# A two-layer flow-matching step: the correcting half of each weight is added from SBUF in convolutions and attention, from DRAM from the LayerNorm to the output projection

## The chip, the cores and the metric

The kernel runs on one core of a Trainium2 chip. The metric is the device time of one execution in microseconds (us), lower is better. The kernel before took 2286.52 us (median of 3 runs, 2286.14 to 2286.73).

## What is computed

Two layers of a backbone with four parallel branches (a Conformer convolution, a Hyena long convolution by FFT, a pooling mixer and grouped-query attention), on 128 context tokens and 512 latent tokens, all in float32. Cut to what matters here: nearly all the time goes into products of the 640 tokens with weight matrices.

```python
def parallel_mixer(h, p, latent, k_ctx, v_ctx):       # h: (1, L, 1024), L = 128 or 512
    u = h @ p['w_in']                                 # 1024 x 11264
    (a_glu, a_gate, b_proj, b_gate, c_in, c_gate,
     q, k, v, d_gate, g_merge) = jnp.split(u, points, axis=-1)
    ya = conformer_conv(a_glu, p['conv_dw_w'], p['conv_dw_b'], p['conv_ln_g'],
                        p['conv_ln_b'], p['conv_pw'])
    ya = (ya * jax.nn.silu(a_gate)) @ p['wo_conv']
    ...
    yb = hyena(b_proj, p['hy_short_w'], p['hy_short_b'], filt, p['hy_skip'])
    yb = (yb * jax.nn.silu(b_gate)) @ p['wo_hyena']
    yc = multiscale_pool(c_in, p['pool_w'], p['pool_scale'])
    yc = (yc * jax.nn.silu(c_gate)) @ p['wo_pool']
    ...
    yd = (att * jax.nn.silu(d_gate)) @ p['wo_attn']
    gm = jax.nn.sigmoid(g_merge).reshape(B, L, N_BRANCH, D_MODEL)
    merged = gm[:, :, 0] * ya + gm[:, :, 1] * yb + gm[:, :, 2] * yc + gm[:, :, 3] * yd
    return merged @ p['w_out'], k, v

def trunk_layer(x, cond, p, latent, k_ctx, v_ctx):
    mod = jax.nn.silu(cond) @ p['w_ada'] + p['b_ada']
    shift, scale, gate = jnp.split(mod, 3, axis=-1)
    h = rms_norm(x, p['norm_g']) * (1.0 + scale) + shift
    y, k, v = parallel_mixer(h, p, latent, k_ctx, v_ctx)
    return x + gate * y, k, v
```

## The kernel before

**Products in three parts.** A float32 number is split into a rounded high part and a remainder, each in the format that TensorE takes at its faster rate, and a product is the sum of three: weight high by activation high, weight high by activation remainder, weight remainder by activation high. Weights come in blocks of at most 128 x 1024 (512 KB). The generator `weights` (L333) makes the two halves of one block: SP loads the block from DRAM into the tile `raw` (L342), ACT casts it into `whi` (L343, in the trace a CAST), and then the remainder `wlo` is made in one of two ways. Where the flag `pooled[0]` is set, ACT writes minus `whi` into `wlo` (L346, an ACTIVATE), and a DMA that POOL issues adds the block to it once more (L347, an *add* below); its source is the weight in DRAM, so that it reads the block a second time, in runs of 512 bytes. Where the flag is not set, VectorE subtracts; that is so for the first three blocks alone, and 269 blocks have an add. `raw` has two buffers, `whi` and `wlo` three each.

**How a block is used.** `proj` (L386) runs, for each half of 320 tokens, 16 matmuls with `whi` and then 8 with `wlo` for a block of 1024 input channels (half as many for 512 channels, 2 and 1 for a block of `pool_w`). The result lies in one of three PSUM banks (`mm`), which ACT or VectorE empties.

**Stages of a layer.** Adaptive modulation; the Hyena branch with its filters, where TensorE runs input projections between the FFT products; values, keys, queries and attention; the merge of the Hyena branch during attention; the convolution's and the pooling branch's inputs; the merge of the attention branch (eight pairs of a `w_in` block and a `wo_attn` block); then `Pooling.gated` (L1737): four pairs of a `w_in` block of 512 KB and a `pool_w` block of 64 KB; the merge of the pooling branch; `Conv.gated` (L1651); the merge of the convolution; the output projection. `Conv.norm` (L1591), the LayerNorm of the convolution, runs on VectorE and ACT beside the attention merge and `Pooling.gated`, and ends inside the latter.

**What sets the order.** The program is written as generators (`lm.spawn`), and a small planner, `Loom`, picks the next one by estimated times; that fixes TensorE's order for good. On the other engines and on the DMA queues of SP and POOL, the tile framework orders the instructions by priority and by its own estimate of when they are ready; each engine then runs its list strictly in order, and waits on semaphores.

Of the kernel before, what the change touches and what calls it, by code (L numbers as in the profile page):

```python
# [10 lines left out]
F32R = mybir.dt.float32r  # L11
I32 = mybir.dt.int32
AF = mybir.ActivationFunctionType
ALU = mybir.AluOpType
# [51 lines left out]
def r32(ap):  # L66
    return ap.bitcast(F32)
# [165 lines left out]
def hybrid_flow_backbone(ctx: ExitStack, tc: tile.TileContext, i, o):  # L233
    nc = tc.nc
# [24 lines left out]
    def nm(p):  # L259
        count[0] += 1  # L260
        return f"{p}{count[0]}"
# [52 lines left out]
    def split(hi, lo, src, scale=None):  # L314
        if scale is None:
            act.copy(hi, src)
            dve.tensor_tensor(out=lo, in0=src, in1=r32(hi), op=ALU.subtract)
        else:
            act.activation(out=hi, in_=src, func=AF.Copy, scale=scale)
            dve.scalar_tensor_tensor(out=lo, in0=src, scalar=scale, in1=r32(hi),  # L320
                                     op0=ALU.mult, op1=ALU.subtract)
# [11 lines left out]
    def weights(src, kk, n):  # L333
        yield from wr.get()
        lm.bg = True
        with tc.high_priority(offset=WAHEAD):
            raw = wp.tile([P, 1024], F32, tag="raw", name=nm("raw"), bufs=NRAW)
            hi = wp.tile([P, 1024], F32R, tag="whi", name=nm("whi"), bufs=NHI)
            lo = wp.tile([P, 1024], F32R, tag="wlo", name=nm("wlo"), bufs=NHI)
            w = kk * n  # L340
            rv = raw[:, 0:w]
            sp.dma_start(out=rv.rearrange("p (k c) -> p k c", k=kk), in_=src)  # L342
            act.copy(hi[:, 0:w], rv)  # L343
            if pooled[0]:

                act.activation(out=lo[:, 0:w], in_=r32(hi[:, 0:w]), func=AF.Copy, scale=-1.0)  # L346
                nc.gpsimd.dma_start(out=lo[:, 0:w].rearrange("p (k c) -> p k c", k=kk), in_=src.bitcast(F32R),  # L347
                                    accum_op=ALU.add)
            else:
                dve.tensor_tensor(out=lo[:, 0:w], in0=rv, in1=r32(hi[:, 0:w]), op=ALU.subtract)  # L350
        lm.bg = False
        return (hi[:, 0:w].rearrange("p (k c) -> p k c", k=kk),
                lo[:, 0:w].rearrange("p (k c) -> p k c", k=kk))

    def w_cols(l, c0):
        return weights(i["w_in"][l][:, c0:c0 + 128].rearrange("(k p) c -> p k c", p=P), 8, 128)
# [18 lines left out]
    def slots(n, dt=F32):  # L375
        r = []
        for _ in range(n):
            r.append((yield from slot(dt)))
        return r

    def new_act(n):
        hi = yield from slots(n, F32R)
        lo = yield from slots(n, F32R)
        return Act(hi, lo)
# [69 lines left out]
    def rsqrt(out, v, n):  # L454

        t = sm.tile([P, 40], F32, tag="rsq_t", name=nm("rt"))[:, 0:n]
        dve.tensor_scalar(out=out.bitcast(I32), in0=v.bitcast(I32), scalar1=1, scalar2=None,
                          op0=ALU.logical_shift_right)
        dve.tensor_scalar(out=out.bitcast(I32), in0=out.bitcast(I32), scalar1=-1.0,
                          scalar2=1597463007.0, op0=ALU.mult, op1=ALU.add)  # L460
        for _ in range(3):
            dve.tensor_tensor(out=t, in0=out, in1=out, op=ALU.mult)
            dve.scalar_tensor_tensor(out=t, in0=t, scalar=-0.5, in1=v, op0=ALU.mult, op1=ALU.mult)
            dve.scalar_tensor_tensor(out=out, in0=t, scalar=1.5, in1=out, op0=ALU.add, op1=ALU.mult)
# [37 lines left out]
    def par(l, ct, row):  # L502
        return prm[:, ct, pcol(l, row):pcol(l, row) + 1]
# [150 lines left out]
    def ada_finish(l, p):  # L654

        ng = prm[:, 2 * (p % 2):2 * (p % 2) + 2, pcol(l, R_NG) + p // 2]
        for cnd in range(2):
            v = mods[l][:, 1, 2 * p:2 * p + 2, cnd]
            dve.scalar_tensor_tensor(out=v, in0=v, scalar=1.0, in1=ng, op0=ALU.add, op1=ALU.mult)
        ev_mod[l][p].set()  # L660
# [10 lines left out]
    def ada_later(jobs, step, start):  # L671
        yield lm.pe + start
        for l, j in jobs:
            yield from ada_chunk(l, j)
            if 4 <= j < 8:
                ada_finish(l, j - 4)
            yield lm.pe + step
# [158 lines left out]
    pooled = [False]  # L836
# [695 lines left out]
    class Conv:  # L1532
# [58 lines left out]
        def norm(self):  # L1591

            l = self.l
            yield self.ev_tap
            co = self.co
            pm = yield from sc.get()
            for j in range(2):
                pe.matmul(pm[:, j, 0:328], lnw.to_broadcast([P, P]), self.pad.v(328 * j, 328), start=True, stop=True)
            self.pad.free()
            for c in range(4):  # L1600
                x = co.v(656 * c, 656)
                xh = x.rearrange("p (a b) -> p a b", a=2)
                yield turn
                dve.tensor_tensor(out=xh, in0=xh, in1=pm[:, :, 0:328], op=ALU.subtract)
            sc.put()
            for c in range(4):
                sq = yield from ur.get(656)
                act.activation(out=sq, in_=co.v(656 * c, 656), func=AF.Square)
                if c == 0:
                    total = sq  # L1610
                else:
                    dve.tensor_tensor(out=total, in0=total, in1=sq, op=ALU.add)
                    ur.put()
            yield lm.sync()
            pvv = yield from ax.get()
            for t in range(5):
                t0 = 0 if t == 0 else 143 + 128 * (t - 1)
                pe.matmul(pvv[:, t:t + 1], total[:, t0:t0 + 128], lnw, start=True, stop=True)
            ur.put(0.0)
            v = sm.tile([P, 5], F32, tag="lnv", name=nm("lnv"))  # L1620
            rs = sm.tile([P, 5], F32, tag="lnr", name=nm("lnr"))
            dve.tensor_scalar(out=v, in0=pvv[:, 0:5], scalar1=EPS, scalar2=None, op0=ALU.add)
            ax.put()
            rsqrt(rs, v, 5)
            yield lm.sync()
            pr = yield from sc.get()
            for t in range(5):
                dst = pr[:, 1, 0:128] if t == 0 else pr[:, 0, 128 * (t - 1):128 * t]
                pe.transpose(dst, rs[:, t:t + 1].to_broadcast([P, P]), ident)
            self.sa = sa = yield from new_act(1)  # L1630
            for c in range(4):
                x = co.v(656 * c, 656)
                xn = yield from ur.get(T)
                dve.tensor_tensor(out=xn[:, 0:128], in0=x[:, 0:128], in1=pr[:, 1, 0:128], op=ALU.mult)
                yield turn
                dve.tensor_tensor(out=xn[:, 128:640], in0=x[:, 143:655], in1=pr[:, 0, :], op=ALU.mult)
                yield turn
                dve.tensor_scalar(out=xn, in0=xn, scalar1=par(l, c, R_LNG), scalar2=par(l, c, R_LNB),
                                  op0=ALU.mult, op1=ALU.add)
                th = yield from ur.get(T)  # L1640
                act.activation(out=th, in_=xn, func=AF.Tanh, scale=0.5)
                yield turn
                dve.scalar_tensor_tensor(out=xn, in0=th, scalar=1.0, in1=xn, op0=ALU.add, op1=ALU.mult)
                ur.put()
                split(sa.h(c), sa.l(c), xn, 0.5)
                ur.put()
            sc.put()
            co.free()
            self.ev_norm.set()

        def gated(self):  # L1651
            l = self.l
# [149 lines left out]
    def layers():  # L1802
# [4 lines left out]
        for l in range(DEPTH):  # L1807
# [74 lines left out]
            if l + 1 < DEPTH:  # L1882
                lm.spawn(late_filters(l + 1, ev_late[l]), 7)
                lm.spawn(ada_later([(1, j) for j in range(8, 12)], 0.0, GS), 50, LATA)
            if l + 1 < DEPTH:
                xT = yield from slots(2)
                evs = [Event(lm) for _ in range(4)]
            yield from out_proj(l, ma, xs, ssq, rows, xT, evs)
            for _ in range(2):
                ur.put()  # L1890
            ma.free()
            if l + 1 < DEPTH:
                yield evs[3]
# [11 lines left out]
    def late_filters(l, ev):  # L1905
        yield ev
        for q in range(2):
            hys[l].threads.append(lm.spawn(hys[l].filters(q), PF0))
# [41 lines left out]
    for x in DORD:  # L1950
# [3 lines left out]
        elif x in "fghi":  # L1954
            c, q = divmod("fghi".index(x), 2)
# [13 lines left out]
    lm.spawn(ada_first(chunks), 3)  # L1969
    lm.spawn(first_sums(*x_first), 4)  # L1970
    lm.spawn(layers(), 6)
    with tc.manual_schedule(engines={mybir.EngineType.PE}):
        lm.run()
# [94 lines left out]
```

## Time and profile before

| what | value |
|---|---|
| runs | 2286.14, 2286.52, 2286.73 us |
| the profiled execution's own time | 2285.64 us |
| its span (first to last instruction) | 2283.8 us, mean granted TensorE clock 0.984 |
| TensorE busy | 2192.5 us (96%) |
| VectorE, ScalarE, GpSimd busy | 58%, 52%, 26% |
| adds (queue q0) | 122.96 MB, 42.4% of the 16 DMA engines' time |
| loads and stores of SP (queue q1) | 186.19 MB, 27.3% |

The profiled execution is 0.9 us under the median. The names in a row of the trace are the kernel's tiles without their numbers: `wlo<-in_w_in_dram` on POOL is an add, `whi<-raw` on ACT a cast, `wlo<-whi` the negated copy, `mm<-sl,wlo` a run of matmuls with a remainder. In a row of a timeline the first number is the start in us from the span's start, the second the duration, and the bracket at the end tells how long the engine was idle before it and what ended that.

### The profile page before, as it was taken

To read this page: it belongs to the slowest core of one execution; us is meant where nothing else is said; L and a number is where in the kernel's file an instruction comes from. 1 tells how busy PE (TensorE), PEld (TensorE's weight loads), DVE (VectorE), ACT (ScalarE), POOL (GpSimd) and SP (SyncE) were. 2 spreads that over 40 slices of the span, in tenths; PEclk is the share of its full clock that TensorE was granted. 3 is DMA by queue.
4 is the path that set the end of the run, shared out by engine and by line. 5 is a ranking of instruction groups with operands and counts; after the bars stand their busy time and mean duration, and the time that the engine had idled before them with its cause. 6 is when DMAs were issued, how large, how long until landed. Compare 5 with 4: busy or idle time off the path is not lost.

```text
span 2283.8 us, 39935 instructions
## 1 busy us (share of the span) xinstructions
PE 2192.5 (96%) x15951; PEld 2145.5 (94%) x15951; DVE 1333.8 (58%) x2762; ACT 1190.4 (52%) x2169; POOL 590.2 (26%) x451
## 2 busy tenths in 40 slices
PE   5999999999999999999997999999999999999999
PEld 3899999999999999999987999999999999999999
DVE  5676786656679944122265777845766897522222
ACT  5544457667654335344564454656776543544442
POOL 2644321101112222222144353111111122222221
PEclk7899999999999999999998999999999999999999
DMA  9376766545568878899973656555455888698986
GB/s 280 104 159 143 163 141 122 101 79 104 109 126 146 151 123 151 150 168 167 226 185 73 109 106 123 105 101 98 82 109 102 150 150 150 113 164 148 173 169 137
DMA packets 508230, 311.83 MB, mean 137 GB/s; under 512 B 12760, under 2 KB 499352, under 8 KB 507789
## 3 DMA queue, kind: packets, MB, share of 16 engines
q0 software_dynamic: 223856, 122.96, 42.4%
q1 hardware_dynamic: 283476, 186.19, 27.3%
q8 instruction: 125, 2.05, 0.4%
q14 instruction: 60, 0.49, 0.1%
q10 hardware_dynamic: 713, 0.14, 0.0%
HBM read 297.02 MB, written 12.22 MB: 135 GB/s over the span
## 4 chain that ended last, share of the span: by engine, by line
PE 74%; issue 9%; DVE 8%; POOL 4%; ACT 3%; DMA 2%; ACTq 0%; SPq 0%; POOLq 0%; DVEq 0%
PE mm L193 58%; PE sc L193 6%; PE ax L193 6%; DVE sl L178 4%; PE ax L202 4%; POOL wlo L347 2%; POOL sl L178 1%; DMA sl<-in_hy_w_dram 1%; DMA wlo<-in_w_in_dram 1%; DVE wx L178 1%; DVE k L178 1%; ACT sl L178 0%; DVE t L178 0%; ACT u L178 0%; DVE u L178 0%
## 5 line engine op out<-in xcount | busy, mean ns | idle before, releaser
L193 PE MATMUL mm<-sl,whi 128*128 128x320 f32 x6304 | 1053.9, 312 | 9.6 <-DVE sl L178 3.9
L193 PEld LDWEIGHTS mm<-sl,whi 128*128 128x128 f32 x6304 | 948.1, 188 | 14.8 <-DVE sl L178 4.5
L193 PE MATMUL mm<-sl,wlo 128*128 128x320 f32 x3152 | 553.7, 311 | 0.9 <-DMA wlo<-in_w_in_dram 0.9
L347 POOL DMA_DIRECT2D wlo<-in_w_in_dram x173 | 264.9, 1531 | 860.2 <-ACT wlo L178 599.5
L193 PEld LDWEIGHTS mm<-sl,wlo 128*128 128x128 f32 x3152 | 483.3, 188 | 1.9 <-DMA wlo<-in_w_in_dram 1.1
L178 ACT CAST whi<-raw 128x1024 fp32r<-128x1024 f32 (+2 forms) x272 | 255.3, 939 | 436.3 <-PE mm L193 423.7
L178 DVE SCALAR_TENSOR_TENSOR t<-t,mm 128x320 f32<-128x320 f32 x192 | 93.2, 486 | 367.7 <-PE mm L193 306.3
L178 ACT ACTIVATE wlo<-whi 128x1024 fp32r<-128x1024 f32 (+2 forms) x269 | 254.9, 948 | 35.6 <-PE mm L193 32.7
L193 PE MATMUL mm<-whi,sl 128*128 128x256 f32 x1600 | 228.8, 286 | 4.2 <-ACT u L178 2.1
L178 DVE SCALAR_TENSOR_TENSOR sc<-sl,prm,sc 128x640 f32<-128x640 f32 (+14 forms) x232 | 207.3, 894 | 12.0 <-ACT sc L178 7.3
L193 PE MATMUL sc<-sl,sl 128*128 128x128 f32 (+1 forms) x1344 | 206.7, 297 | 7.9 <-DVE sl L178 4.2
L193 PEld LDWEIGHTS mm<-whi,sl 128*128 128x128 f32 x1600 | 205.9, 190 | 6.6 <-ACT u L178 2.3
L193 PEld LDWEIGHTS sc<-sl,sl 128*128 128x128 f32 x1344 | 182.3, 196 | 11.3 <-issue 5.5
L178 DVE TENSOR_TENSOR h<-ax,h 128x512 fp32r<-128x512 f32 (+1 forms) x200 | 120.3, 604 | 114.7 <-ACT h L178 113.0
L178 ACT ACTIVATE t<-mm 128x320 f32<-128x320 f32 x208 | 89.8, 432 | 145.9 <-PE mm L193 143.1
L178 DVE TENSOR_SCALAR_CACHE_REDUCE u<-sc,rq 128x640 f32<-128x640 f32 x128 | 112.6, 880 | 44.7 <-PE sc L193 43.8
L193 PE MATMUL mm<-wlo,sl 128*128 128x256 f32 x800 | 128.3, 283 | 5.5 <-DMA wlo<-in_w_in_dram 4.0
L178 ACT ACTIVATE u<-u,nb 128x640 f32<-128x640 f32 x128 | 106.2, 830 | 49.9 <-DVE u L178 49.3
L178 ACT CAST h<-ax 128x512 fp32r<-128x512 f32 (+1 forms) x200 | 102.5, 514 | 52.3 <-PE ax L202 49.9
L193 PE MATMUL ax<-h,sl 128*128 128x256 f32 (+1 forms) x656 | 121.7, 297 | 5.0 <-DVE h L178 3.8
L202 PE MATMUL ax<-ident,u 128*128 128x128 f32 x752 | 118.6, 273 | 3.6 <-DVE h L178 2.0
L193 PEld LDWEIGHTS mm<-wlo,sl 128*128 128x128 f32 x800 | 109.3, 190 | 6.3 <-DMA wlo<-in_w_in_dram 4.5
(213 smaller groups left out, 2232.9 us busy)
## 6 DMA issues: line engine op xcount, KB each, us to landing
raw<-in_w_in_dram SPq DMA_DIRECT2D x176, 512.0 KB
wlo<-in_w_in_dram POOLq DMA_DIRECT2D x173, 512.0 KB, 6.5
wlo<-in_w_ada_dram SPq DMA_DIRECT2D x19, 512.0 KB
whi<-in_w_ada_dram SPq DMA_DIRECT2D x19, 512.0 KB
raw<-in_wo_attn_dram SPq DMA_DIRECT2D x16, 512.0 KB
wlo<-in_wo_attn_dram POOLq DMA_DIRECT2D x16, 512.0 KB, 6.3
raw<-in_w_out_dram SPq DMA_DIRECT2D x16, 512.0 KB
wlo<-in_w_out_dram POOLq DMA_DIRECT2D x16, 512.0 KB, 7.2
```

The source lines that it names most:

```text
L178: r = f(*args, **kw)
L193: r = self.real.matmul(out, lhsT, rhs, **kw)
L202: r = self.real.transpose(out, in_, ident)
L347: nc.gpsimd.dma_start(out=lo[:, 0:w].rearrange("p (k c) -> p k c", k=kk), in_=src.bitcast(F32R), accum_op=ALU.add)
```

## The change

The flag gets a third value. At 1 (or True) the add takes the block from `raw` in SBUF, as one run of up to 4096 bytes a partition; at 2 from DRAM, as before. It is set to 2 at the end of `Conv.norm` and ahead of the output projection, and to 1 after the output projection.

```diff
@@ in weights @@
-                nc.gpsimd.dma_start(out=lo[:, 0:w].rearrange("p (k c) -> p k c", k=kk), in_=src.bitcast(F32R),
-                                    accum_op=ALU.add)
+                if pooled[0] == 2:
+                    nc.gpsimd.dma_start(out=lo[:, 0:w].rearrange("p (k c) -> p k c", k=kk), in_=src.bitcast(F32R),
+                                        accum_op=ALU.add)
+                else:
+                    nc.gpsimd.dma_start(out=r32(lo[:, 0:w]), in_=rv, accum_op=ALU.add)
@@ at the end of Conv.norm @@
             self.ev_norm.set()
+            pooled[0] = 2
@@ in layers, around the output projection @@
+            pooled[0] = 2
             if l + 1 < DEPTH:
                 xT = yield from slots(2)
                 evs = [Event(lm) for _ in range(4)]
             yield from out_proj(l, ma, xs, ssq, rows, xT, evs)
             for _ in range(2):
                 ur.put()
+            pooled[0] = 1
```

Of the 269 adds, 175 get their source from `raw`: in each layer all up to the first `w_in` block behind `Pooling.gated`. The order of TensorE stays as it was, row by row. On ACT and SP some rows move. Below, a row with - stands there in the kernel before, a row with + in the changed one. In what follows the third and the fourth `w_in` block of `Pooling.gated` of the first layer are called A and B, the first two `w_in` blocks of the merge behind it C and D. Their tiles: `raw_9488` (A), `raw_9578`, `whi_9579`, `wlo_9580` (B), `raw_9668`, `whi_9669`, `wlo_9670` (C), `raw_9776`, `whi_9777`, `wlo_9778` (D).

ACT around the cast of B (`u` and `sl_9338` belong to the LayerNorm, `sl_9166<-t_9398` is a gated result of the pooling branch):

```order
 L178 ACTIVATE sl_9338<-u_9605 128x640
+L178 ACTIVATE u_9729<-u_9695 128x640
 L178 CAST whi_9579<-raw_9578 128x1024
-L178 ACTIVATE u_9729<-u_9695 128x640
+L178 ACTIVATE sl_9166<-t_9398 128x640
 L178 ACTIVATE wlo_9580<-whi_9579 128x1024
-L178 ACTIVATE sl_9166<-t_9398 128x640
 L178 ACTIVATE sl_9338<-u_9695 128x640
```

The cast of B goes behind one ACT operation, and another one stands between it and the negated copy.

ACT around the cast of C (`t_9577<-mm_9585` empties the PSUM bank of B's first half of tokens; `whi_9740` is the first `wo_pool` block):

```order
+L178 ACTIVATE sl_9166<-t_9487 128x640
 L178 CAST whi_9669<-raw_9668 128x1024
 L178 ACTIVATE wlo_9670<-whi_9669 128x1024
-L178 ACTIVATE sl_9166<-t_9487 128x640
 L178 ACTIVATE t_9577<-mm_9585 128x320
 L178 CAST whi_9740<-raw_9739 128x512
 L178 ACTIVATE wlo_9741<-whi_9740 128x512
 L178 ACTIVATE t_9577<-mm_9617 128x320
+L178 ACTIVATE sl_9166<-t_9577 128x640
 L178 CAST whi_9777<-raw_9776 128x1024
 L178 ACTIVATE wlo_9778<-whi_9777 128x1024
-L178 ACTIVATE sl_9166<-t_9577 128x640
```

Only the gated results move; the emptying of B's banks stands behind the cast and the copy of C, and of the `wo_pool` block, in both kernels.

SP in the same stretch (`u` are small rows of the output gate, `raw_9739` is the first `wo_pool` block):

```order
-L342 DMA raw_9739<-in_wo_pool_dram 128x4x128
 L325 DMA u_10856<-grow 125x256
 L325 DMA u_10856<-grow 2x256
 L325 DMA u_10856<-in_b_ada_dram 1x256
 L325 DMA u_10856<-grow 125x256
+L342 DMA raw_9668<-in_w_in_dram 128x8x128
+L342 DMA raw_9739<-in_wo_pool_dram 128x4x128
 L342 DMA raw_9776<-in_w_in_dram 128x8x128
```

The load of C, which stood among the first of twelve small loads, comes behind all of them.

## Rows read from the trace of the kernel before

**Rows 1.** Page, part 1: busy time and share of each engine.

```profile
PE 2192.5 (96%) x15951; PEld 2145.5 (94%) x15951; DVE 1333.8 (58%) x2762; ACT 1190.4 (52%) x2169; POOL 590.2 (26%) x451
```

**Rows 2.** Waits of TensorE: who, for whom; us in total, times, longest.

```profile
PE mm L193 <- DMA wlo<-in_w_in_dram: 4.9, 3, 3.0
```

**Rows 3.** Timeline of TensorE, two of these waits.

```profile
305.27 0.74 PE L193 MATMUL mm<-wlo,sl 128*128 128x256 f32 x4 [1.04 <-DMA wlo<-in_w_in_dram]
...
1550.91 1.22 PE L193 MATMUL mm<-wlo,sl 128*128 128x256 f32 x4 [3.00 <-DMA wlo<-in_w_in_dram]
```

**Rows 4.** Groups of POOL's instructions: count, busy us, mean ns, idle before.

```profile
L347 POOL DMA_DIRECT2D wlo<-in_pool_w_dram x8 | 7.2, 896 | 45.6 <-ACT wlo L178 45.6
```

**Rows 5.** DMA issues: count, KB each, median us from issue to landing.

```profile
wlo<-in_w_in_dram POOLq DMA_DIRECT2D x173, 512.0 KB, 6.5
...
wlo<-in_pool_w_dram POOLq DMA_DIRECT2D x8, 64.0 KB, 2.7
```

**Rows 6.** Table by stretch: busy us, clock, DMA share, GB/s (last).

```profile
1381.20:1382.50 1.30, 1.30 (x12) 1.30 (x11) 1.30 (x3) 0.64 (x1) 0.00 (x0) 1.00 1.22 196
...
1729.50:1730.50 1.00, 1.00 (x11) 1.00 (x8) 1.00 (x2) 1.00 (x2) 0.00 (x0) 1.00 0.66 173
1730.50:1731.50 1.00, 1.00 (x10) 0.99 (x9) 0.88 (x4) 0.97 (x3) 0.90 (x1) 1.00 1.01 303
1731.50:1732.00 0.50, 0.50 (x6) 0.50 (x5) 0.27 (x1) 0.48 (x3) 0.50 (x1) 1.00 0.28 83
```

**Rows 7.** Timeline of SP: a load that ran alone, and the load of B.

```profile
862.64 0.37 SPq L342 DMA_DIRECT2D raw<-in_w_in_dram  x1
...
1728.50 0.37 SPq L342 DMA_DIRECT2D raw<-in_w_in_dram  x1
```

**Rows 8.** Timeline of POOL and of ACT in the attention merge.

```profile
807.95 1.58 POOL L347 DMA_DIRECT2D wlo<-in_w_in_dram  x1
...
819.37 1.05 ACT L178 CAST whi<-raw 128x1024 fp32r<-128x1024 f32 x1 [4.46 <-PE mm L193]
```

**Rows 9.** Timeline of POOL: the adds of A and B.

```profile
864.57 1.57 POOL L347 DMA_DIRECT2D wlo<-in_w_in_dram  x1 [2.03 <-ACT wlo L178]
...
873.62 1.59 POOL L347 DMA_DIRECT2D wlo<-in_w_in_dram  x1 [2.77 <-ACT wlo L178]
```

**Rows 10.** Timeline of ACT: B's cast, negated copy, pooling result; C's; B's bank.

```profile
870.51 1.04 ACT L178 CAST whi<-raw 128x1024 fp32r<-128x1024 f32 x1
...
872.09 1.04 ACT L178 ACTIVATE wlo<-whi 128x1024 fp32r<-128x1024 f32 x1
873.04 0.72 ACT L178 ACTIVATE sl<-t 128x640 fp32r<-128x640 f32 x1
...
878.69 1.05 ACT L178 CAST whi<-raw 128x1024 fp32r<-128x1024 f32 x1
879.77 1.06 ACT L178 ACTIVATE wlo<-whi 128x1024 fp32r<-128x1024 f32 x1
...
882.91 0.44 ACT L178 ACTIVATE t<-mm 128x320 f32<-128x320 f32 x1 [1.45 <-PE mm L193]
```

**Rows 11.** Timeline of TensorE: remainders of B, last pool_w product, C, remainders of C, D.

```profile
881.53 1.34 PE L193 MATMUL mm<-sl,wlo 128*128 128x320 f32 x8
...
886.70 0.46 PE L193 MATMUL mm<-sl,whi 128*128 128x320 f32 x2
...
887.60 2.61 PE L193 MATMUL mm<-sl,whi 128*128 128x320 f32 x16 [0.30 <-ACT t L178]
890.04 1.34 PE L193 MATMUL mm<-sl,wlo 128*128 128x320 f32 x8
...
900.65 1.34 PE L193 MATMUL mm<-sl,wlo 128*128 128x320 f32 x8
```

**Rows 12.** Timeline of VectorE: the gate that frees the PSUM bank behind ACT.

```profile
883.38 0.49 DVE L178 SCALAR_TENSOR_TENSOR t<-t,mm 128x320 f32<-128x320 f32 x1 [1.06 <-ACT t L178]
```

## The prediction, made before the changed kernel ran

> **What bounds the kernel now.** I read the page's first part first: TensorE is busy for 2192.5 us of a span of 2283.8 us, 96%, and no other engine is above 58% [rows 1]. So the change can gain only where TensorE waits for an add, and can lose only where an add, or what an add holds up, comes too late. The second view is that of TensorE's waits: the sum of its waits for adds of `w_in` blocks is 4.9 us in three waits, the longest 3.0 us [rows 2]. The reader is to see how small that is beside 173 such adds [rows 5]. The timeline shows two of the three: 1.04 us ahead of 305.27 and 3.00 us ahead of 1550.91 [rows 3]. The third view is that of the DMA issues, which gives the time from issue to landing: 6.5 us for a 512 KB add [rows 5]. With the gain bounded at 4.9 us, the question is whether the new source makes another wait.
>
> **POOL's issues.** 175 adds have one run a partition instead of 1024 runs of 512 bytes in all for a `w_in` block. The nearest row is the add of a `pool_w` block, 128 runs, which keeps POOL for 896 ns [rows 4]; a `w_in` add keeps it for 1.57 to 1.59 us [rows 9]. That is 0.68 us less for an add, at most 175 x 0.68 = 119 us of POOL. POOL is busy 26% of the span [rows 1], and TensorE's row of waits names the landing, not POOL, so I cost this at nothing on the path. If that cover is gone, it is a gain, and a rival below.
>
> **The landing.** No row shows an add out of SBUF. A bound from above is no change at all, 6.5 us. For the rest I start from the `pool_w` add, which has as many runs and 64 KB, and lands 2.7 us after its issue [rows 5]. A `w_in` add moves 448 KiB (459 KB) more. In a stretch where only an add of another kind of block moved bytes, in runs of 1 KB, the rate was 196 GB/s [rows 6] (first line): 459 / 196 = 2.3 us, 5.0 in all. At the best rate of a plain load, 303 GB/s [rows 6] (third line), it would be 1.5 us and 4.2 in all. I take 4.9, an estimate close to the first, since an add is nearer to an add than to a load, and runs of 4 KB should be a little better than runs of 1 KB. The ends for the range are 4.1 and 6.4.
>
> The Trainium skill has another figure: its page "DMA: Bandwidth & Descriptors", section "Anatomy of one DMA — SWDGE (gpsimd) path", fits such a transfer by 2.0 us and the bytes at 436 GB/s, an estimate of 3.2 us for 512 KB. The trace of before does not agree, with its 6.5 us [rows 5]; by the page the loss worked out below would vanish and the time be near 2284 us.
>
> **The buffer that is now held.** This is the part that the change adds. Until now `raw` was free when the cast and the subtraction no longer needed it: the next load into a buffer waited for a cast only. Now the add itself reads `raw`, so the load of the block after next waits in SP's list until the add has landed, and everything behind it in that list waits too. A load that runs alone is issued at 1728.50 [rows 7], its bytes run until 1732.0 [rows 6] (last lines), and I give it 0.3 us to be seen: 3.8 us. The cycle of one `raw` buffer becomes: cast to negated copy 1.1, negated copy to add 1.5 (872.09 to 873.62) [rows 9, 10], landing 4.9, load 3.8, in all 11.3 us.
>
> In the merge of the attention branch this is hidden. The add issued at 807.95 would land at 812.9, the load behind it at 816.7, and the cast that needs this load starts at 819.37, since it waits for TensorE to free `whi` [rows 8]. That leaves 2.7 us, and 1.2 even at 6.4. In the earlier stages casts wait for TensorE likewise. Small loads that stand behind a late `raw` load in SP's list I cost at nothing: what they bring is used much later. If that cover went, an SP delay of a few us would show as waits in the conditioning or the scratch stores.
>
> In `Pooling.gated` it is not hidden. `pool_w` blocks lie between the `w_in` blocks, so all four `w_in` blocks take the same one of two buffers, and TensorE uses up a pair in 8.5 us (B's remainders at 881.53, C's at 890.04) [rows 11], less than 11.3. Step by step in the first layer:
>
> A's add at 864.57 [rows 9] lands at 869.5. B's load, which was issued at 862.64 [rows 7], goes then and lands at 873.3; its cast starts then instead of at 870.51 [rows 10]. A gated result of the pooling branch (0.72 us [rows 10]) now stands between cast and negated copy: copy 875.0, add 876.45, landing 881.35. TensorE needs it at 881.53 [rows 11]: no stall, by 0.2 us.
>
> C's load at 881.4 lands at 885.2; its cast starts at 885.2 instead of 878.69 [rows 10], copy 886.3, add 887.75, landing 892.65. But ACT's emptying of B's bank, at 882.91 today [rows 10], stands behind C's copy: it comes at 887.35, takes 0.44, then VectorE's 0.49 [rows 12], so that the bank is free at 888.4 and the last `pool_w` product, today at 886.70, is 1.7 us late. The cast and copy of the `wo_pool` block stand before the next emptying, and C's first product comes at about 890.1 instead of 887.60 [rows 11]: 2.5 late. C's remainders are then due at 892.6, about when the add lands: 2.6 us late.
>
> D's add takes DRAM again, but D's load must wait for C's add: issued 892.7, landed 896.5, add 899.05, landed 6.4 later at 905.5. TensorE needs it at 900.65 [rows 11] + 2.6 = 903.25: another 2.3. From here the cycle is as before and has time to recover. The sum is 4.9, say 5 us for a layer. The second layer has the same order there: 10 us for both.
>
> **What is gained.** The wait of 1.04 us at 305 goes, as the add lands 1.6 us sooner; the wait of 3.00 us at 1550.91 shrinks; I take 1.0 of it, less than the 1.6 by which the median landing falls, since the add there may be among the quicker ones. Some 2 us. What is late next there is the same add.
>
> **The sum.** The profiled execution took 2285.6 us, 0.9 under the median of 2286.5. 2285.6 + 10 - 2 is 2293.6; rounded, **2294 us**. At a landing of 4.1 the cycle is 10.5, the loss by the same steps 2.4 a layer and the gain 2.6: 2285.6 + 4.8 - 2.6 = 2287.8. At 6.4 the steps give 9.5 a layer and no gain: 2304.6. About 0.2%, 4.6 us, is what a measurement of this kernel can tell from no change.
>
> **The rivals.** *The adds out of SBUF are quick, and the two effects cancel* (2284 to 2289). For it: 128 runs instead of 1024. Against it: even the 64 KB add takes 2.7 us [rows 5], and the cycle must fall to 8.5 us for no loss, a landing of 2.1. In between it is a small loss against a gain of at most 4.9 [rows 2]. Chance 0.27.
>
> *The source makes no difference*, so that the change does not do what it says: an add reads, sums and writes at the pace of its SBUF side, 6.4 us, and only holds `raw` longer. For it: in an add alone, with 1 KB runs, the engines were full at 196 GB/s [rows 6]. About 2303. Chance 0.10.
>
> *POOL is relieved where TensorE depends on it* (faster). In the Hyena stages POOL computes parts of the filters behind adds in its list; an issue shorter by 0.68 us moves each such operation forward if it stands directly behind an add and a product waits for it. I count some 16 such operations in the two filter chains: at most 11 us, less what the pooling stages lose if the adds there land quickly; at a landing near 4.1 some 8 of them decide the sign, and 2285.6 - 11 + 4.8 - 2.6 is about 2277; a part of them, 2280. Against it: POOL's share of 26% [rows 1]. Chance 0.11 that it brings the time under 2282.
>
> **How the numbers follow.** Forecast 0.52 (own range 2290 to 2299), quick adds 0.27, no difference 0.10, POOL 0.11. Slower by over 0.2% holds the forecast less a small part near its lower end, and the third case: 0.58. Within 0.2% (2282 to 2291) is the second case and that part, 0.30. Faster is 0.12. The range 2284 to 2303 leaves out the faster case and the far end of the third.
>
> **What would show it.** In the profile after: POOL's issue of a `w_in` add near 0.9 us and its landing near 4.9; SP's loads of `raw` waiting for an add where they waited for a cast; in `Pooling.gated` of each layer the casts of B and C waiting for a load, the emptying of B's bank some 4 us later, and two waits of TensorE of 2 to 3 us each, for a PSUM bank or C's add, then for D's; the attention merge as today. The forecast is wrong if adds land within 4.1 us or after 6, or if TensorE has no new waits there; and if the time falls by more than 2 us, then the gain lies in a place that I did not price.

## The result and the profile after

The changed kernel took 2303.15 us (median of 4 runs, 2299.81 to 2306.84), the kernel before 2286.62 us: a ratio of 1.0075 with a 95% interval of 1.0061 to 1.0088. It is slower, as forecast, but by 16.5 us instead of 7.5, and lies just outside the range. Its four runs lie 7.0 us apart and the four of the kernel before 0.7, but four runs say little of scatter: in the experiments below the kernel before scattered by 4.2 to 5.1 us over 13 to 27 runs. The profiled execution took 2305.26 us, 2.1 over the median, with a span of 2303.5 us against 2283.8, so that the trace has 19.7 us to explain.

The page's first part answers to [rows 1]. TensorE has the same 15951 matmuls; POOL is busy 107.6 us less:

```profile
PE 2200.8 (96%) x15951; PEld 2148.2 (93%) x15951; DVE 1331.7 (58%) x2762; ACT 1188.4 (52%) x2169; POOL 482.6 (21%) x451
```

The DMA issues (count, KB each, median us from issue to landing) and POOL's group answer to [rows 4, 5]:

```profile
wlo<-raw POOLq DMA_DIRECT2D x151, 512.0 KB, 4.7
wlo<-in_w_in_dram POOLq DMA_DIRECT2D x38, 512.0 KB, 6.6
...
wlo<-raw POOLq DMA_DIRECT2D x8, 64.0 KB, 3.2
```

```profile
L351 POOL DMA_DIRECT2D wlo<-raw x175 | 151.5, 866 | 1154.5 <-ACT wlo L178 840.3
```

The two prices that no row of before showed were near: a landing of 4.7 us (forecast 4.9), an issue of 866 ns (forecast 896). Yet TensorE's waits for adds, 4.9 us before [rows 2], became 9.2, and the waits for a bank that VectorE empties (`t`) 7.2 us, from 3.0:

```profile
PE mm L193 <- DMA wlo<-raw: 7.5, 5, 2.9
PE mm L193 <- DVE t L178: 7.2, 9, 1.8
...
PE mm L193 <- DMA wlo<-in_w_in_dram: 1.7, 3, 1.2
```

The same view of the kernel before has for `t`:

```profile
PE mm L193 <- DVE t L178: 3.0, 7, 1.0
```

TensorE's order is the same in both kernels, so the start of the same instruction in the two traces tells where time went. From the timelines of TensorE:

| instruction | before | after | later by |
|---|---|---|---|
| first of 16 FFT products `sc`, first layer | 169.78 | 171.22 | 1.4 |
| input projection behind them | 174.09 | 178.41 | 4.3 |
| transposes of the keys (`ax<-ident,k` x5) | 328.62 | 334.30 | 5.7 |
| B's first product, first layer | 879.09 | 886.41 | 7.3 |
| D's first product, first layer | 898.30 | 914.07 | 15.8 |
| transpose ahead of the wait for `w_ada` | 1185.06 | 1201.71 | 16.7 |
| product with that `w_ada` block | 1186.88 | 1205.79 | 18.9 |
| product ahead of a filter of the second layer | 1314.61 | 1333.98 | 19.4 |
| product behind it | 1320.39 | 1337.53 | 17.1 |
| remainder awaited for 3.00 us before [rows 3] | 1550.91 | 1566.09 | 15.2 |
| B's first product, second layer | 1998.00 | 2011.95 | 14.0 |
| `w_in` block behind D, second layer | 2027.64 | 2047.75 | 20.1 |
| end | 2283.8 | 2303.5 | 19.7 |

Three things are to be seen. From B to D the first layer loses 8.5 us and from B to behind D the second loses 6.1: 14.6 of the 19.7. Outside, the first layer and the conditioning of the second lose about 11. And from 1318 to 1998 some 5 are won back.

**Pooling.gated, first layer.** SP, ACT, POOL and TensorE in turn (start, duration, and in the bracket the idle time before and its end):

```profile
876.75 0.37 SPq L342 DMA_DIRECT2D raw<-in_w_in_dram  x1
...
882.08 0.61 SPq L325 DMA_DIRECT2D u<-grow  x2
...
891.88 0.39 SPq L342 DMA_DIRECT2D raw<-in_w_in_dram  x1
...
898.98 0.37 SPq L342 DMA_DIRECT2D raw<-in_w_in_dram  x1
904.16 0.37 SPq L342 DMA_DIRECT2D raw<-in_wo_pool_dram  x1
```

```profile
880.76 1.05 ACT L178 CAST whi<-raw 128x1024 fp32r<-128x1024 f32 x1 [2.21 <-DMA raw<-in_w_in_dram]
...
882.36 1.04 ACT L178 ACTIVATE wlo<-whi 128x1024 fp32r<-128x1024 f32 x1
...
895.98 1.05 ACT L178 CAST whi<-raw 128x1024 fp32r<-128x1024 f32 x1 [7.88 <-DMA raw<-in_w_in_dram]
...
898.03 0.42 ACT L178 ACTIVATE t<-mm 128x320 f32<-128x320 f32 x1
898.34 0.61 ACT L178 CAST whi<-raw 128x512 fp32r<-128x512 f32 x1
```

```profile
871.79 0.86 POOL L351 DMA_DIRECT2D wlo<-raw  x1 [1.99 <-ACT wlo L178]
...
883.69 0.86 POOL L351 DMA_DIRECT2D wlo<-raw  x1 [5.57 <-ACT wlo L178]
...
898.41 0.86 POOL L351 DMA_DIRECT2D wlo<-raw  x1 [11.63 <-ACT wlo L178]
```

```profile
886.41 2.58 PE L193 MATMUL mm<-sl,whi 128*128 128x320 f32 x16 [0.30 <-DVE t L178]
891.88 1.44 PE L193 MATMUL mm<-sl,wlo 128*128 128x320 f32 x8 [2.88 <-DMA wlo<-raw]
...
899.02 0.56 PE L193 MATMUL mm<-sl,whi 128*128 128x320 f32 x2 [1.74 <-DVE t L178]
...
904.19 2.38 PE L193 MATMUL mm<-sl,wlo 128*128 128x320 f32 x8 [1.82 <-DMA wlo<-raw]
```

SP's loads of B and C (876.75, 891.88) go as soon as the add of the block before has landed (876.69, 891.83), the casts wait for them, and the emptying of B's bank at 898.03 stands behind C's copy, as forecast. D's load does not wait for C's add, as the prediction had it: it goes at 898.98, when ACT is done with the cast of the first `wo_pool` block (898.34), 5.2 us before C's add lands at 904.15. The load that waits for C's add is that of the second `wo_pool` block, at 904.16. What was not forecast is the first wait of TensorE: B's add, issued at 883.69, landed at 891.83, after 8.1 us, where A's took 4.9. The table by stretch (us; busy time of TensorE, its weight loads, VectorE, ACT, POOL; granted clock; DMA share; GB/s) shows how it ends:

```profile
886.00:888.00 2.00, 1.70 (x12) 1.62 (x12) 1.21 (x3) 0.64 (x1) 0.78 (x1) 1.00 0.98 198
888.00:890.00 2.00, 1.00 (x7) 0.74 (x6) 0.82 (x1) 0.10 (x1) 0.00 (x0) 1.00 0.47 94
890.00:892.00 2.00, 0.12 (x1) 0.13 (x2) 0.00 (x0) 0.00 (x0) 0.00 (x0) 1.00 0.10 16
```

The mean busy share of the sixteen DMA engines is 0.47 from 888 and 0.10 from 890, so that only a few can still be at work at the end of the add. Around it the small loads of the output gate go (`u<-grow`), in each layer four of 125 rows. Three of them are issued within 2.2 us here (882.08 to 884.21), because the `pool_w` load ahead of them (881.34) waited for an add to land (881.29). In the kernel before, the four are spread from 872.48 to 878.87.

The waits are not all: behind those at 899.02 and 904.19 the granted clock fell to 0.51 from 904.4 to 907.8 (the lower of the two levels, 1.2 GHz), and the products there took 1.6 us longer. In the second layer the same happened from 2023.9 to 2027.2, for 1.4 us:

```profile
2023.19 4.00 PE L193 MATMUL mm<-sl,whi 128*128 128x320 f32 x16
```

So some 3 us of the 14.6 are clock and not waits.

### The profile page after: what moved, and what is told of

Read it like the earlier page. It is cut to its first block, busy times and chain, and to the rows that moved or that the text cites. A ratio compares the mean times of both kernels' runs of the same rounds, so it can differ in the third digit from the quotient of the medians.

```text
span 2303.5 us, 40021 instructions
## 1 busy us (share of the span) xinstructions
PE 2200.8 (96%) x15951; PEld 2148.2 (93%) x15951; DVE 1331.7 (58%) x2762; ACT 1188.4 (52%) x2169; POOL 482.6 (21%) x451
## 4 chain that ended last, share of the span: by engine, by line
PE 64%; issue 12%; DVE 10%; DMA 6%; POOL 5%; ACT 3%; ACTq 0%; POOLq 0%; SPq 0%; DVEq 0%
PE mm L193 49%; PE sc L193 6%; PE ax L193 5%; DVE sl L178 5%; PE ax L202 4%; POOL wlo L348 3%; DMA wlo<-raw 2%; DMA wlo<-in_w_in_dram 1%; DVE wx L178 1%; DMA raw<-in_w_in_dram 1%; POOL sl L178 1%; DVE k L178 1%; DMA sl<-in_hy_w_dram 1%; ACT sl L178 1%; ACT u L178 1%
## 5 line engine op out<-in xcount | busy, mean ns | idle before, releaser
L351 POOL DMA_DIRECT2D wlo<-raw x175 | 151.5, 866 | 1154.5 <-ACT wlo L178 840.3
```

Source lines behind the costliest of these rows:

```text
L351: nc.gpsimd.dma_start(out=r32(lo[:, 0:w]), in_=rv, accum_op=ALU.add)
```

## The experiments

Theories, and what tells them apart: **H**, the held `raw` buffer costs its time in `Pooling.gated`; **S**, the SBUF source costs wherever it is used; **R**, the small loads delay B's add; then, on the rest of the program, **G** (a quicker add gains where TensorE waits for it), **L** (the first layer's early stages lose time) and **K** (a `raw` load that is held back gets in front of a load that TensorE awaits). The edits choose blocks by `wc[0]`, a counter of the blocks in the order of their creation, 0 to 271; the two lines that count are not shown, and where a condition changes, the line replaced is the one shown in e1. All ratios are to runs of the kernel before on the same chip (medians 2286.3 to 2287.0).

### e1: the stretch around Pooling.gated from DRAM

```diff
-                if pooled[0] == 2:
+                if not (pooled[0] != 2 and not (wc[0] in range(80, 89) or wc[0] in range(216, 225))):
```

> The change, but the 18 adds of the stretch around Pooling.gated (blocks 80 to 88 and 216 to 224, counted in order of creation) take DRAM again. Theory H (the raw buffer held until an add lands costs time in Pooling.gated): in the changed profile TensorE loses 8.5 us in that stretch of the first layer and 6.1 in the second; both go, and 2303 falls by about 14, to 2286 to 2291. Rival S (an SBUF source costs something wherever it is used, some 0.1 us for each of 175 adds): only 18 of 175 are taken back, 2300 to 2302.

Measured: 2289.12 us, ratio 1.0014 (1.0005 to 1.0023). In its trace TensorE loses 0.3 us in the first stretch and nothing in the second. With 18 of 175 adds taken back, 14 us are gone; S falls. It is still not the 2284 that a gain of 2 us outside would give: the other 157 adds cost about 3 us together.

### e2: an SBUF source there alone

```diff
+                if not (wc[0] in range(80, 89) or wc[0] in range(216, 225)):
```

> The kernel before, with an SBUF source for those 18 adds alone. Theory H: the two stretches lose 14 us by themselves, 2286.5 + 14 = 2300 (2296 to 2302). Rival S: 2286.5 + 2 = 2288 or 2289.

Measured: 2297.0 us, ratio 1.0047 (1.0034 to 1.006), 10.7 us over the kernel before. TensorE's waits there, second layer:

```profile
2007.13 1.44 PE L193 MATMUL mm<-sl,wlo 128*128 128x320 f32 x8 [1.11 <-DMA wlo<-raw]
...
2014.19 0.56 PE L193 MATMUL mm<-sl,whi 128*128 128x320 f32 x2 [1.66 <-DVE t L178]
...
2019.21 1.44 PE L193 MATMUL mm<-sl,wlo 128*128 128x320 f32 x8 [1.66 <-DMA wlo<-raw]
...
2030.87 1.43 PE L193 MATMUL mm<-sl,wlo 128*128 128x320 f32 x8 [0.84 <-DMA wlo<-in_w_in_dram]
```

These are the places of the forecast, C's bank, C's add and D's, with B's add in front (6.5 us to land here). H stands. By TensorE's starts the two stretches lose 6.6 and 6.1 us, 12.7 in all.

### e3: the source kept, the hold spread

```diff
-            raw = wp.tile([P, 1024], F32, tag="raw", name=nm("raw"), bufs=NRAW)
+            if n == 128 and kk == 1:
+                raw = hp.tile([P, 1024], F32, tag="h0", name=nm("raw"))
+            else:
+                raw = wp.tile([P, 1024], F32, tag="raw", name=nm("raw"), bufs=NRAW)
```

> The change, but the pool_w blocks load into a tile of another pool, so that the w_in blocks of Pooling.gated alternate between the two raw buffers; all 175 adds stay on SBUF. Theory H: the hold is spread over two buffers (cycle 11.3 us against 17 us for two pairs), so most of the 14 us goes, 2288 to 2293, and no wait of TensorE for an add is left there but perhaps B's. Rival S, or any price of the SBUF source itself: still 2300 to 2304.

Measured: 2292.57 us, ratio 1.0024 (1.0014 to 1.0034). All 175 adds are still from SBUF, and 10.6 of the 16.5 us are gone. B's and C's adds are no longer awaited; what is left is D. Here, unlike in the changed kernel, its load does wait for C's add (landed at 893.73, load at 893.78), because `w_in` and `wo_pool` blocks take turns on the two buffers there:

```profile
893.49 2.60 PE L193 MATMUL mm<-sl,whi 128*128 128x320 f32 x16 [0.30 <-ACT t L178]
...
908.88 1.33 PE L193 MATMUL mm<-sl,wlo 128*128 128x320 f32 x7 [2.18 <-DMA wlo<-in_w_in_dram]
```

The row at 893.49 is C's first product, with no more than the usual 0.30 us ahead of it [rows 11]. So it is the hold and not the source. D costs 4.0 us in the first layer, of which some 1.6 are a fall of the clock behind its wait, and 1.4 in the second.

### e4: without the small loads

```diff
+            if n % 2 == 0:
+                dve.memset(t, 0.0)
             load(r[n][0:2], grow[l, n][0:2])
             load(r[n][2:3], i["b_ada"][l:l + 1, 2048 + 256 * n:2304 + 256 * n])
-            load(r[n][3:P], grow[l, n][3:P])
```

> The change without the eight loads of 125 rows of the output gate (two of the tiles are set to zero by VectorE, so the gate of the output is computed from three of its 128 partial rows). These loads run beside B's add in Pooling.gated. Theory R (B's add lands in 8.1 and 6.0 us instead of 4.5 because these small loads keep some DMA engines busy): B's add lands in 4.5 to 5 us, TensorE's wait of 2.9 us (first layer) and 0.6 us (second) for it goes, and what follows is early by as much; 2303 falls by 3 to 6, to 2297 to 2300. Rival Q (B's add shares POOL's queue with the pool_w add issued 2.2 us later): B's landing stays at 6 to 8 us, the time at 2302 to 2304.

This leaves out rows that the output gate sums, so the run is for its time alone. Measured: 2297.71 us, ratio 1.0046 (1.0034 to 1.0059), 5.4 us under the changed kernel. B's add landed 4.55 us after its issue in both layers (from 8.1 and 6.0), and TensorE does not wait for it any more. In the first layer this is left:

```profile
885.10 2.59 PE L193 MATMUL mm<-sl,whi 128*128 128x320 f32 x16 [0.30 <-DVE t L178]
894.29 0.56 PE L193 MATMUL mm<-sl,whi 128*128 128x320 f32 x2 [1.45 <-DVE t L178]
899.31 1.45 PE L193 MATMUL mm<-sl,wlo 128*128 128x320 f32 x8 [1.67 <-DMA wlo<-raw]
911.54 1.45 PE L193 MATMUL mm<-sl,wlo 128*128 128x320 f32 x8 [1.35 <-DMA wlo<-in_w_in_dram]
```

R stands, Q falls: the `pool_w` add is still issued 2.4 us behind B's. Of the 5.4 us, B's two waits are 3.5 (2.88 and 0.64); the rest fits the clock, which does not fall in either stretch here. TensorE loses 5.0 us in this stretch and 4.0 in the second layer. That the forecast had 4.9 is in part luck: with a landing of 4.55 its own steps give some 3.7. C's add took 5.6 us in both layers, though the small loads were gone (893.68 to 899.27 here; POOL issues the DRAM add of a `wo_pool` block 1.5 us behind it), and D's load took 7.0 us to its cast, beside these two adds, instead of 3.8.

### e5 and e6: where an add is awaited, and nothing else

```diff
+                if not (wc[0] in range(145, 172)):
```

> The kernel before, with an SBUF source for 27 adds alone: blocks 145 to 171, the last input projections of the second layer's Hyena branch and its values, keys and queries. Theory G (where TensorE waits for an add or for something that an add delays, the quicker add gains; the raw buffer is not missed, since casts there wait for TensorE): in the changed profile TensorE gains 2.2 us about 1318, loses some 0.5 at 1370, gains 1.6 about 1440 and 1.2 to 2.4 about 1551; alone that is 2286.3 - 4 to - 5.5 = 2281 to 2282.5. Rival N (those gains follow from what came before in the changed kernel, such as a clock that fell at another place, and not from the add): 2285 to 2287.

Measured: 2284.6 us, ratio 0.9988 (0.9979 to 0.9997), 2.4 us faster than the kernel before, and so faster than both. G stands by its sign, though not by its size: in the trace the gains at 1318 (1.6 us) and 1551 (2.3 us) come, the one at 1440 does not. In e6 block 20 is added to it:

> As e5, and one add more from SBUF: block 20, whose add TensorE awaits for 1.04 us at 305 in the kernel before. Theory G: that wait goes and no load is late, as its raw buffer's next load has 6 us to spare; 1 us under e5, 2280 to 2281.5. Rival N: as e5, no difference.

Measured: 2284.32 us, ratio 0.9992 (0.9983 to 1.0001): no gain over e5. The profiled execution was the slowest of its eleven (2290.70 us), so that the trace serves for this one place and not for the total. TensorE does not wait at 305 any more and is 1.3 us earlier; but the next thing it waits for is a result of VectorE (`k`), which is not earlier. Of before and of e6:

```profile
325.49 0.44 PE L202 MATMUL ax<-ident,k 128*128 128x128 f32 x2 [1.42 <-DVE k L178]
```

```profile
325.82 0.44 PE L202 MATMUL ax<-ident,k 128*128 128x128 f32 x2 [2.13 <-DVE k L178]
326.01 1.60 PE L193 MATMUL mm<-whi,sl 128*128 128x256 f32 x8
```

The wait grew from 1.42 to 2.13 us and starts the transposes no sooner; the products behind it then ran at half the clock for a while (granted 0.50 from 327.4 to 330.0, the level of 1.2 GHz, where the kernel before had 1.00). e1's trace shows the same without a fall of the clock: 1.2 us won at 304, 1.1 lost at 325.

### e7: the first layer's first part alone

```diff
+                if not (wc[0] in range(3, 25)):
```

> The kernel before, with an SBUF source for blocks 3 to 24 alone (22 adds: the first layer's Hyena inputs, values, keys, queries). Theory L (the changed kernel loses time here too: VectorE's operations meet POOL's, which begin at other times, a load held back makes ACT wait in front of other work, and the clock falls after one of the longer idle stretches): as in the profiles of the change, +1.2 about 140, +1.7 to 3.2 about 170, -1.3 at 305, +1.2 to 2.6 about 322, in all +3 to +5: 2289 to 2291.5. Rival M (these are the scatter of single executions): 2285 to 2287.

Measured: 2291.66 us (2286.09 to 2301.6), ratio 1.0021 (1.0009 to 1.0033), 4.7 us slower. L stands in its total: by the trace it loses 1.25 us about 140, 1.9 about 170 and 2.6 about 322, and wins 1.3 at 305. The three are not equally sure. The 1.25 us come in all six kernels with these blocks from SBUF and in none of the others. Of the 1.9 us at 170, 1.6 are a fall of the clock, which came in e6 too, where these adds but one take DRAM, and not in e8, where all take SBUF; so this part belongs to the execution as much as to the change. The 2.6 us at 322 are e6's, behind the win at 305. Where the first of these comes from shows in VectorE's and POOL's timelines, before and after the change:

```profile
138.32 0.88 DVE L178 TENSOR_TENSOR sl<-sl 128x512 f32<-128x512 f32 x2
...
139.15 1.29 POOL L178 TENSOR_TENSOR k<-k,k 128x512 f32<-128x512 f32 x1 [4.84 <-ACT k L178]
```

```profile
138.77 1.98 DVE L178 TENSOR_TENSOR sl<-sl 128x512 f32<-128x512 f32 x2
...
138.96 1.64 POOL L178 TENSOR_TENSOR k<-k,k 128x512 f32<-128x512 f32 x1 [5.55 <-ACT k L178]
```

VectorE's pair takes 1.98 us instead of 0.88, where POOL's operation starts in the middle of it and not at its end. The Trainium skill, page "SBUF — State Buffer", section "SBUF: two separate sides", says that VectorE, in an operation with two SBUF inputs, and GpSimd share one pair of ports, which one of them holds for a whole instruction while the other blocks; this trace agrees, with 1.1 us more for the pair and 0.35 more for POOL. By what way the change moved the two against each other (POOL's shorter issues, later loads) no run here tells apart.

### e8: all adds from SBUF

> All 269 adds take SBUF. Theory H (the hold of raw costs wherever its cycle is longer than TensorE's time for the blocks between): in the merges of the pooling and the convolution branch a w_in and a wo block take turns, each its own raw buffer, and TensorE takes 10.6 us for a pair; the cycle there is 1.1 to the copy, 1.4 to the add, 4.5 to the landing, 3.8 to the load, 10.8 us and more where ACT is busy, so that each of some 28 pairs loses 0.2 to 1 us: 2308 to 2330. Rival: the hold matters in Pooling.gated alone, 2300 to 2305.

Measured: 2344.17 us, ratio 1.025 (1.0236 to 1.0264), 57 us slower and far over the expectation. TensorE's two largest new waits are those of the hold, and they come again and again through the merges:

```profile
PE mm L193 <- DVE t L178: 16.8, 17, 6.0
PE mm L193 <- DMA wlo<-raw: 13.9, 18, 2.2
```

The direction is H's; the size was underestimated. By TensorE's starts, `Pooling.gated` loses 4.6 and 4.4 us, the stages from there to the output projection 21.6 and 15.1, 1.3 for each of the 28 pairs, and the output projections, which the expectation did not price, 5.7 and 5.3.

### e9: one add

```diff
+                if not (wc[0] == 136):
```

> The kernel before, with an SBUF source for a single add, that of block 136 (the first w_in block of the second layer). Theory K (a held raw buffer also turns up in SP's list, where a late load of raw goes just ahead of loads that TensorE awaits): the load of block 138, at 1170.9 us in the kernel before, goes only when that add has landed, at about 1182.4, right ahead of two loads of w_ada of 512 KB each; these land some 2 us later, and TensorE loses 1.8 to 2.6 us at 1187, where the five kernels that keep this block on SBUF lost 2.1 to 2.9; 2288 to 2289. Rival: that loss came from work shifted earlier in the program; without it TensorE is at 1187 within 0.6 us of the kernel before, 2286 to 2287.

Measured: 2289.21 us, ratio 1.0009 (1.0000 to 1.0019), 2.2 us slower from a single add, at the edge of what its ten runs can tell from nothing. SP before and in e9, then TensorE in both:

```profile
1170.88 0.38 SPq L342 DMA_DIRECT2D raw<-in_w_in_dram  x1
...
1182.40 0.37 SPq L620 DMA_DIRECT2D whi<-in_w_ada_dram  x1
```

```profile
1182.44 0.37 SPq L344 DMA_DIRECT2D raw<-in_w_in_dram  x1
1182.91 0.53 SPq L625 DMA_DIRECT2D whi<-in_w_ada_dram  x1
```

```profile
1186.88 0.64 PE L193 MATMUL ax<-whi,cs 128*32 128x256 f32 x8 [1.55 <-DMA whi<-in_w_ada_dram]
```

```profile
1189.25 1.08 PE L193 MATMUL ax<-whi,cs 128*32 128x256 f32 x8 [4.12 <-DMA whi<-in_w_ada_dram]
```

K stands for this wait. The load of `raw`, held for 11.6 us until the add of block 136 landed at 1182.43, goes 0.47 us ahead of the `w_ada` load that TensorE awaits. The wait grows by 2.57 us; the clock is halved already for the next products (1.08 us instead of 0.64), while in the kernel before it fell 1.8 us behind their start. What it costs the program is less sure: by 1250 TensorE is only 1.2 us later than in the kernel before, and this profiled execution as a whole took 2285.22 us, no longer than that one's.

## Why the prediction was wrong

**What bounds the kernel, the gain's bound, the prices.** The prices were right: landing 4.7 instead of 4.9, issue 866 ns instead of 896. The bound was not quite: "only where TensorE waits for an add" leaves out 1318, where TensorE waits for ACT and VectorE, and where 2.2 us were gained (1.6 in e5).

**The hold in Pooling.gated.** That a held `raw` buffer makes TensorE wait there was right, and so were the first steps. In the changed kernel it costs 14.6 us and not 10, and the step that failed is the landing: one landing time, 4.9, was used for all adds of a size. Taking off the 7.3 us by which the stretch begins later, B's cast came at 873.4 (forecast 873.3), its copy at 875.0 (875.0), its add at 876.4 (876.45); its landing came at 884.5 instead of 881.35, and C's cast at 888.7, 3.5 late with it. B's add took longer than the median already in the kernel before: issued at 873.62 [rows 9], it lands at 880.65, after 7.0 us against 6.5 [rows 5], beside the same small loads. This was in the trace and was not read. C's add landed after 5.7 and 5.6 us. And the clock, which fell in both stretches for some 3 us, has no term in the sum.

**"D's load must wait for C's add."** It does not, in the changed kernel, e2 or e4: it goes when the cast of the first `wo_pool` block is done, and so takes that block's buffer. D came late all the same, because its load took 6.9 us to the cast (898.98 to 905.91) where the sum has 3.8; beside it ran C's add and a `wo_pool` add (issued at 898.41 and 899.91), and which of them slowed it no run tells apart. TensorE waited 1.2 us for D in the second layer and not at all in the first, where the slowed products covered it; the forecast had 2.3 in each.

That e2 costs 10.7 us, against the 10 of the forecast, is therefore luck in part: its two stretches lose 12.7, with 2.3 for B's adds (forecast nothing) and 2.2 for D's (forecast 4.6).

**"Small loads that stand behind a late raw load I cost at nothing."** This failed twice. In `Pooling.gated` it was not their lateness but their company that cost: in e4, without them, B's add lands after 4.55 us and its waits of 3.5 us are gone. And at 1187 the late one was not small: a `w_ada` load of 512 KB that TensorE awaits lost 2.3 us (16.7 to 18.9 in the table; 2.6 in e9). The prediction looked at how late those loads would be issued and not at what would then go just ahead of them.

**"In the earlier stages casts wait for TensorE likewise."** For the buffers this was true, but the conclusion, no loss, was not: e7 is 4.7 us slower. VectorE and POOL meet in another order (1.25 us), and TensorE's clock fell at two places where it had not in the kernel before.

**The gain of 2 us.** The wait at 305 went and was given back 20 us later, because VectorE's result was due next, and not the add (e6). The wait of 3.00 us shrank by 1.1, as forecast. Two more gains came that were not priced: at 1318, where TensorE waited 1.14 and 0.56 us for a filter's values from ACT and VectorE (why these came earlier was not tested), and behind 1551. By e5 they are worth 2.4 us, if no other add changes.

**The sum.** In the profiled execution -2 outside `Pooling.gated` was +5 and +10 inside was +14.6. Of the rivals none came true. The one by which the source makes no difference has the measured time, about 2303, but by luck: it wanted adds that land after 6.4 us, and they landed after 4.7. POOL's relief, meant as a gain, may be behind the loss at 140; no run shows that.

## What to carry to other kernels

Where a transfer reads a buffer instead of memory, cost first the buffer: its cycle (cast, copy, issue, landing, load) against the consumer's time, stage by stage; a stage with a shorter period than the cycle pays, however quick the transfer is, and a spare buffer there (e3) takes most of it away. Take the landing and the load of the very place from the trace and not the median of all, and look up which buffer each load really takes. In each queue through which the later reload passes, look at what comes right behind it: one load in front of an awaited one made a wait 2.6 us longer. And price a gain only up to the next wait on another engine.

## What the runs showed of the hardware

Of the 151 adds of 512 KB in runs of 4 KB out of SBUF in the changed kernel, 90 landed after 4.5 to 4.9 us and 50 after more than 5.2, the slowest after 8.75. Beside the small loads of 125 rows B's took 8.1 and 6.0 us (94 and then 16 GB/s at the end of the first), and 4.55 us in both layers without them (e4). The quickest, 4.47 us, disagrees with the fit that the prediction cited from the Trainium skill, page "DMA: Bandwidth & Descriptors", section "Anatomy of one DMA — SWDGE (gpsimd) path" (an estimate of 3.2 us by it).

TensorE's clock fell at places where it had not in the kernel before. At 168.0 to 171.2 the idle time before the FFT products was 2.63 us instead of 2.32, and behind it the granted clock was 0.50, the 1.2 GHz level:

```profile
168.00:171.20 3.20, 0.58 (x4) 0.33 (x4) 3.20 (x7) 0.00 (x0) 0.93 (x2) 0.89 0.63 131
171.20:175.00 3.80, 3.78 (x18) 3.80 (x19) 1.87 (x5) 0.00 (x0) 0.00 (x0) 0.50 0.34 72
```

It is not a matter of the last wait alone. At this place the clock fell in five of the six kernels that idled 2.60 to 2.65 us, but not in e8 (2.63 us), and of the five that idled 2.30 to 2.35 it fell in e6 (2.31 us). In the changed kernel the products ran on at full rate behind the 2.88 us at 891.88, and behind the 1.82 us at 904.19 they did not (2.38 us for 8 products instead of 1.34). A fall cost 1.4 to 2.9 us at these places, and its place differs between executions of the same instructions: the clock was low from 21.3 for 20.5 us in the kernel before and in e5, and not there in e2 and e9, whose instructions up to there are the same. That may be a part of the scatter of the runs; how large a part stays open.
